# A Strassen-form input projection for a hybrid decoder trunk on one Trainium2 core

## The chip, the cores and the metric

The kernel runs on one core of a Trainium2 chip. The metric is the device time of one execution in microseconds (us); the number compared is the median over several runs. A profiled execution gives the trace. PE is the tensor engine, DVE the vector engine, ACT the scalar engine, POOL the GpSimd engine, and SP the engine that issues most transfers.

## What is computed

One layer and a final norm, in float32, for 512 tokens (`SEQ`) of width 2048 (`D_MODEL`):

```python
h = rmsnorm(x, norm_g)
proj = h @ w_in                      # 2048 x 15360
a_u, a_b, a_c, a_z, b_v, b_g, b_z, c_u, c_z, gates = split(proj)   # nine of 1024, then 6144
y_a = (silu(a_z) * (a_b * causal_dwconv3(a_c * a_u))) @ w_br_a     # 1024 x 2048
v = causal_dwconv31(b_v * sigmoid(b_g)) + conv_b
y_b = (silu(b_z) * silu(layernorm(v))) @ w_br_b
y_c = (silu(c_z) * (grouped(pooled(c_u) - c_u) * scale)) @ w_br_c  # windows 2, 4, 8, 16
g = sigmoid(gates)                                                 # three of 2048
x = x + (g0 * y_a + g1 * y_b + g2 * y_c) @ w_o                     # 2048 x 2048
return rmsnorm(x, final_g)
```

The input projection is 2048 x 15360 per token, the three branch projections are 1024 x 2048 each, and the output projection is 2048 x 2048.

## The kernel before

Every product is made in three passes. Both operands are cut into a part of 12 significant bits (`h`) and the exact rest (`l`), and the tensor engine adds `h*h`, `h*l` and `l*h` into one PSUM bank. For the weights this cut is done on the chip, chunk by chunk: a chunk is 128 x 512 numbers, ACT copies it to `wh` (L79) and DVE subtracts that from the raw chunk to give `wl` (L80). The class `Weights` runs ahead of the use: raw units of two chunks (512 KB) are loaded by the SP queue (L66) into three buffers, and the parts lie in four buffers for each of `wh` and `wl`. There are 644 chunks, each used for 12 matmuls of 512 columns.

The input projection is made with channels on the partitions. `product(x)` (L175) makes one tile of 128 channels by 512 tokens: the weight chunk is the stationary operand, 128 x 128 at a time, and the 16 tiles of `x` (as `xh`, `xl`) move past it. So a tile costs 16 x 3 = 48 matmuls, and the 120 tiles of the projection cost 5760. Channels on the partitions are what the convolutions along tokens and the per-channel parameters need, so nothing has to be turned. The reciprocal root of the mean square, which varies along tokens, is a row `R` spread over all partitions.

The order is: the head (the first four tiles, while `x` comes in), branch B up to its gate, branch A with its gates and its projection, branch B's gate and projection, branch C, and the output projection, which is made with tokens on the partitions (L479 to L481: `mh`, `ml` are stationary and the weight chunk moves). The long convolution (31 taps on DVE, L264) is put into a queue `todo` as 31 tasks a tile; `feed` takes one or two of them after each weight chunk, so they run beside the matmuls of the following products. All intermediate results stay in SBUF. The last column group of the output is made token tile by token tile, so that only one tile's norm, scaling and store lie behind the last matmul.

The order on each engine is set by a scheduler that follows the order of the program, with a priority for the cuts of the weights.

Of the kernel before, what the change touches and what calls it, by code (L numbers as in the profile page):

```python
# [19 lines left out]
NT = S // P  # L20
CONV_A = 3
# [6 lines left out]
UNIT = 2 * CH  # L28
# [3 lines left out]
# Column offsets of the segments of the input projection, in tiles of 128.  # L32
A_U, A_B, A_C, A_Z, B_V, B_G, B_Z, C_U, C_Z, GATE = (KB * i for i in range(10))

# Columns of the packed per-channel parameters.
# [9 lines left out]
HEAD = (B_V, B_G, B_V + 1, B_G + 1)  # L45


class Weights:
    """The weights in the order of their use: raw tiles are loaded ahead, and split ahead into a
    part of 12 significant bits and the exact rest, which the tensor engine takes in one pass each."""  # L50

    def __init__(self, tc, nc, raw, parts, src, load_ahead, split_ahead):
        self.tc, self.nc, self.raw, self.parts, self.src = tc, nc, raw, parts, src
        self.load_ahead, self.split_ahead = load_ahead, split_ahead
        self.fine = 1
        self.units, self.chunks = {}, {}
        self.n_units = src.shape[0]
        self.loaded = self.split = self.at = 0

    def load_to(self, n):  # L60
        while self.loaded < min(n, self.n_units):
            u = self.loaded
            t = self.raw.tile([P, UNIT], F32, tag="raw", name=f"raw{u}")
            for i in range(0, UNIT, CH if u < self.fine else UNIT):
                at = slice(i, i + (CH if u < self.fine else UNIT))
                self.nc.sync.dma_start(out=t[:, at], in_=self.src[u][:, at])  # L66
            self.units[u] = t
            self.loaded += 1

    def split_to(self, n):  # L70
        while self.split < min(n, 2 * self.n_units):
            c = self.split
            self.load_to(c // 2 + 1 + self.load_ahead)
            raw = self.units[c // 2][:, (c % 2) * CH : (c % 2 + 1) * CH]
            pool, tag = self.place(c)
            h = pool.tile([P, CH], F32R, tag=tag or "wh", name=f"wh{c}")
            l = pool.tile([P, CH], F32R, tag=tag or "wl", name=f"wl{c}")
# [4 lines left out]
            if c % 2:  # L82
                del self.units[c // 2]
            self.split += 1

    def place(self, c):
        return self.parts, None
# [8 lines left out]
def trunk(ctx: ExitStack, tc: tile.TileContext, xT, xn, wts, par, fg, out):  # L96
    nc = tc.nc
    const = ctx.enter_context(tc.tile_pool(name="const", bufs=1))
    xp = ctx.enter_context(tc.tile_pool(name="xp", bufs=2 * KD))
    up = ctx.enter_context(tc.tile_pool(name="up", bufs=2 * KB))  # L100
    vp = ctx.enter_context(tc.tile_pool(name="vp", bufs=2 * KB))
    mp = ctx.enter_context(tc.tile_pool(name="mp", bufs=KD))
    raw = ctx.enter_context(tc.tile_pool(name="raw", bufs=3))
    parts = ctx.enter_context(tc.tile_pool(name="parts", bufs=4))
    tp = ctx.enter_context(tc.tile_pool(name="tp", bufs=6))
    sp = ctx.enter_context(tc.tile_pool(name="sp", bufs=4))
# [9 lines left out]
    def tmp():  # L116
        return tp.tile([P, S], F32, tag="t", name=nm("t"))

    def psum():
        return ps.tile([P, S], F32, tag="ps", name=nm("ps"))  # L120

    def small():
        return sp.tile([P, 1], F32, tag="s", name=nm("s"), bufs=16)

    # ---- loads of the start
    gcol = const.tile([P, KD], F32, name="gcol")
    nc.scalar.dma_start(out=gcol, in_=par[:, P_G : P_G + KD])
    prm = const.tile([P, NPAR], F32, name="prm")
    xraw = []
    w = Weights(tc, nc, raw, parts, wts, 2, 3)  # L130
    for k in range(KD):
        t = mp.tile([P, S], F32, tag="m", name=f"xraw{k}")
        nc.sync.dma_start(out=t, in_=xT[:, k, :])
        xraw.append(t)
        w.load_to({0: 1, 2: 2, 4: 3}.get(k, 0))
        if k == KD - 1:
            nc.sync.dma_start(out=prm, in_=par)
# [5 lines left out]
    # The activation table and the tensor engine's full clock are had before the first data arrive.  # L143
# [4 lines left out]
    # 1 / (t + 1), for the first positions, where a window is cut off.  # L148
# [3 lines left out]

    def row(name):
        return const.tile([P, S], F32, tag="row", name=name, bufs=D // S)

    R, R2, acc, a = row("R"), row("R2"), row("squares"), row("meansq")
# [4 lines left out]
    # ---- work for the other engines that is fed in between the matrix products  # L161
    todo = deque()
    rate = [1]

    def feed(n):
        for _ in range(min(n, len(todo))):
            todo.popleft()()

    def mm3(p, whl, cols, ahl, first, last):
        (wh, wl), (ah, al) = whl, ahl  # L170
        T.matmul(p, lhsT=wh[:, cols], rhs=ah, start=first, stop=False)  # L171
        T.matmul(p, lhsT=wh[:, cols], rhs=al, start=False, stop=False)  # L172
        T.matmul(p, lhsT=wl[:, cols], rhs=ah, start=False, stop=last)  # L173
# [54 lines left out]
    for k in range(KD):  # L228
# [7 lines left out]
        for i, p in enumerate(head):  # L236
            mm3(p, whl, slice(i * P, (i + 1) * P), x[k], k == 0, k == KD - 1)
# [355 lines left out]
```

## Time and profile before

| | us |
|---|---|
| median of 3 runs | 1771.6 (1771.44 to 1772.04) |
| span of the profiled execution | 1770.0 |
| PE busy | 1759.4 (99%) |
| DVE busy | 911.4 (51%) |
| ACT busy | 530.8 (30%) |

The profiled execution's own span, from its first to its last instruction, is 1770.0 us, which is 1.6 us under the median of the runs. Matmuls overlap in the records, so the busy time of PE is the union of them; the time that one matmul takes of the engine is the distance from one start to the next.

### The profile page before, as it was taken

How to read it: one execution, taken by the hardware profiler on the slowest of the kernel's cores; microseconds unless marked ns; L12 is line 12 of the kernel's file. 1: busy time of each engine (PE TensorE's matmuls, PEld its weight loads, DVE VectorE, ACT ScalarE, POOL GpSimd, SP SyncE). 2: the span in 40 equal slices, each digit the busy share in tenths (PEclk: the TensorE clock that was granted, in tenths of full speed). 3: DMA queues.
4: the chain of work that ended last, by engine and by line, in shares of the span. 5: the costliest groups of instructions: out<-in, count | busy, mean ns of one | idle time of the engine just before them, and what ended most of it. 6: DMA issues, size and time to landing. Idle time of an engine off the chain costs nothing.

```text
span 1770.0 us, 19981 instructions
## 1 busy us (share of the span) xinstructions
PE 1759.4 (99%) x7798; PEld 1459.7 (82%) x7798; DVE 911.4 (51%) x1478; ACT 530.8 (30%) x878; POOL 0.2 (0%) x4
## 2 busy tenths in 40 slices
PE   9999999999999999999999999999999999999998
PEld 7888888888888888888888888888888888888887
DVE  7899999544443367334433333345553333363343
ACT  6322222222222234223322222233332222242232
POOL 0000000000000000000000000000000000000000
PEclk9999999999999999999999999999999999999999
DMA  6333322332232322333322233322333332262342
GB/s 229 97 98 104 95 96 96 99 102 96 96 101 96 95 96 95 102 100 97 95 96 95 96 97 102 99 96 95 96 96 96 101 100 96 96 196 95 97 130 96
DMA packets 54383, 183.93 MB, mean 104 GB/s; under 512 B 6160, under 2 KB 6288, under 8 KB 54288
## 3 DMA queue, kind: packets, MB, share of 16 engines
q1 hardware_dynamic: 50112, 175.30, 30.6%
q10 hardware_dynamic: 4176, 7.35, 1.3%
q8 instruction: 61, 1.00, 0.2%
q14 instruction: 34, 0.28, 0.0%
HBM read 178.43 MB, written 4.19 MB: 103 GB/s over the span
## 4 chain that ended last, share of the span: by engine, by line
PE 99%; DMA 0%; ACT 0%; DVE 0%; issue 0%
PE ps L171 30%; PE ps L172 30%; PE ps L173 30%; PE ps L479 2%; PE ps L480 2%; PE ps L481 2%; PE ps L496 1%; PE ps L497 1%; PE ps L498 1%; DMA xraw<-xT 0%; ACT y L509 0%; PE ps L201 0%; PE ps L200 0%; ACT squares L239 0%; ACT xh L232 0%
## 5 line engine op out<-in xcount | busy, mean ns | idle before, releaser
L80 DVE TENSOR_TENSOR wl<-raw,wh 128x512 fp32r<-128x512 f32 x644 | 443.1, 689 | 596.7 <-ACT wh L79 590.5
L171 PE MATMUL ps<-xh,wh 128*128 128x512 f32 x1920 | 746.0, 390 | 1.1 <-ACT wh L79 1.1
L172 PE MATMUL ps<-xl,wh 128*128 128x512 f32 x1920 | 747.0, 390 | 0.0
L79 ACT CAST wh<-raw 128x512 fp32r<-128x512 f32 x644 | 399.6, 622 | 1154.8 <-PE ps L172 1023.6
L173 PE MATMUL ps<-xh,wl 128*128 128x512 f32 x1920 | 741.8, 389 | 0.0
L171 PEld LDWEIGHTS ps<-xh,wh 128*128 128x128 f32 x1920 | 361.0, 188 | 76.0 <-ACT wh L79 1.4
L172 PEld LDWEIGHTS ps<-xl,wh 128*128 128x128 f32 x1920 | 361.2, 188 | 75.0
L173 PEld LDWEIGHTS ps<-xh,wl 128*128 128x128 f32 x1920 | 360.7, 188 | 74.7
L264 DVE SCALAR_TENSOR_TENSOR conv<-v,prm,conv 128x497 f32<-128x497 f32 (+25 forms) x240 | 165.1, 735 | 0.0
L481 PE MATMUL ps<-wl,mh 128*128 128x512 f32 x192 | 74.8, 390 | 0.0
L479 PE MATMUL ps<-wh,mh 128*128 128x512 f32 x192 | 74.8, 390 | 0.0
L480 PE MATMUL ps<-wh,ml 128*128 128x512 f32 x192 | 74.8, 389 | 0.0
L375 DVE TENSOR_TENSOR t<-ps,R 128x512 f32<-128x512 f32 x48 | 33.2, 692 | 73.6 <-PE ps L173 73.6
L172 PE MATMUL ps<-ucl,wh 128*128 128x512 f32 x144 | 56.1, 389 | 0.0
L173 PE MATMUL ps<-uch,wl 128*128 128x512 f32 x144 | 56.1, 389 | 0.0
L171 PE MATMUL ps<-uch,wh 128*128 128x512 f32 x144 | 56.1, 389 | 0.0
L171 PE MATMUL ps<-uah,wh 128*128 128x512 f32 x128 | 49.9, 390 | 0.0
L171 PE MATMUL ps<-ubh,wh 128*128 128x512 f32 x128 | 49.9, 390 | 0.0
L173 PE MATMUL ps<-uah,wl 128*128 128x512 f32 x128 | 49.9, 389 | 0.0
L172 PE MATMUL ps<-ubl,wh 128*128 128x512 f32 x128 | 49.9, 389 | 0.0
L173 PE MATMUL ps<-ubh,wl 128*128 128x512 f32 x128 | 49.9, 389 | 0.0
L172 PE MATMUL ps<-ual,wh 128*128 128x512 f32 x128 | 49.8, 389 | 0.0
(119 smaller groups left out, 940.3 us busy)
## 6 DMA issues: line engine op xcount, KB each, us to landing
raw<-wts SPq DMA_DIRECT2D x321, 512.0 KB, 3.4
xraw<-xT SPq DMA_DIRECT2D x16, 256.0 KB, 5.8
y<-xn ACTq DMA_DIRECT2D x16, 256.0 KB, 5.4
out<-y SPq DMA_DIRECT2D x8, 256.0 KB, 3.2
out<-y ACTq DMA_DIRECT2D x8, 256.0 KB, 3.8
fgb<-fg ACTq DMA_DIRECT2D x4, 256.0 KB, 4.3
raw<-wts SPq DMA_DIRECT2D x2, 256.0 KB, 4.3
prm<-par SPq DMA_DIRECT2D x1, 160.0 KB, 4.9
```

The source lines that it names most:

```text
L79: self.nc.scalar.copy(out=h, in_=raw)
L80: self.nc.vector.tensor_tensor(out=l, in0=raw, in1=h.bitcast(F32), op=ALU.subtract)
L171: T.matmul(p, lhsT=wh[:, cols], rhs=ah, start=first, stop=False)
L172: T.matmul(p, lhsT=wh[:, cols], rhs=al, start=False, stop=False)
L173: T.matmul(p, lhsT=wl[:, cols], rhs=ah, start=False, stop=last)
L264: V.scalar_tensor_tensor(out=c[:, s:], in0=v[:, : S - s], scalar=pcol(P_BW, i * CONV_B + CONV_B - 1 - s), in1=c[:, s:], op0=ALU.mult, op1= ...
L375: V.tensor_tensor(out=g, in0=p, in1=R, op=ALU.mult)
L479: T.matmul(pt[t], lhsT=mh[:, tk], rhs=h, start=k == 0, stop=False)
L480: T.matmul(pt[t], lhsT=ml[:, tk], rhs=h, start=False, stop=False)
L481: T.matmul(pt[t], lhsT=mh[:, tk], rhs=l, start=False, stop=k == KD - 1)
L496: T.matmul(p, lhsT=mh[:, tk], rhs=h[:, at], start=k == 0, stop=False)
L497: T.matmul(p, lhsT=ml[:, tk], rhs=h[:, at], start=False, stop=False)
```

## The change

The 15360 columns of the projection are made in 15 units of two 512-column halves (left and right). For each unit `x` (tokens by 2048) and the weights (2048 by 1024) are seen as 2 x 2 blocks: two halves of the tokens, two halves of the input channels, the left and the right columns. Strassen's form (Winograd's variant) makes the four result blocks from seven block products, where the plain form takes eight.

- The operands from `x` (`make`, `operand`) are built once, during the first unit: seven of eight tiles each, for 256 tokens, with the `h` part in the left and the `l` part in the right half of one tile. They stay in SBUF and are the stationary operand; the weight chunks move.
- Of the seven weight operands two are plain loads into the pools `A` and `C`, one is a plain load into `B`, and four are made in place: a DMA issued by POOL adds a block of the weights to the raw buffer that the product before has used (`accum_op=ALU.add`). A unit has 28 raw stages of 512 KB, 12 loaded and 16 added. An add can go out only when both chunks that lay in the buffer have been cut.
- A chunk of the projection is now used for 6 matmuls (two token tiles, three passes). 500 stages give 1000 chunks to be cut, where there were 644.
- The results come out with tokens on the partitions. ACT saves a bank where a partial sum is needed later (`snap`), DVE joins it with a later bank (`join`). What needs channels on the partitions is turned by PE, four 128 x 128 transposes a tile (`turned`): 64 tiles, 256 transposes.
- Gates, convolution inputs and outputs, `cu`, `cz` and `z` are stored to DRAM by the ACT queue (`spill`) and loaded back by the SP queue (`fill`), 256 KB each.
- The queue of side tasks is fed 0.75 tasks per chunk during the projection (1.0 in the first unit and after the projection). Turns go before the other tasks.
- The mean squares of the tokens are made from a second copy of the input, `xn`, on ACT (`square`).
- All 15 units come first, then the three branch projections with the gated sum, now with tokens on the partitions, then the turn of the sum and the output projection.

The diff, cut to its core (`branch`, the convolution, the LayerNorm and the pooling are moved and fed from DRAM, with the same arithmetic):

```diff
+PRODUCTS = (
+    ("11", "A", "load", 0, 0),
+    ("s1", "A", "add", 0, 1),
+    ("s2", "A", "add", 1, 1),
+    ("s4", "B", "load", 1, 1),
+    ("s3", "B", "add", 0, 1),
+    ("12", "C", "load", 1, 0),
+    ("22", "A", "add", 1, 0),
+)
+STEPS = KD // 4
...
     def load_to(self, n):
...
+        while self.loaded < min(n, len(self.stages)):
+            tag, key, what, b = self.stages[self.loaded]
+            if what == "load":
+                t = self.pools[tag].tile([P, RAW], F32, tag=tag, name=f"raw{tag}{self.loaded}")
+                self.nc.sync.dma_start(out=t, in_=self.src[b])
+                self.raw[key] = t, self.loaded
+            else:
+                t, before = self.raw[key]
+                assert self.split >= 2 * before + 2
+                self.nc.gpsimd.dma_start(out=t, in_=self.src[b], accum_op=ALU.add)
...
-    raw = ctx.enter_context(tc.tile_pool(name="raw", bufs=3))
-    parts = ctx.enter_context(tc.tile_pool(name="parts", bufs=4))
+    ra = ctx.enter_context(tc.tile_pool(name="ra", bufs=STEPS))
+    rb = ctx.enter_context(tc.tile_pool(name="rb", bufs=STEPS))
+    rc = ctx.enter_context(tc.tile_pool(name="rc", bufs=2))
+    parts = ctx.enter_context(tc.tile_pool(name="parts", bufs=5))
+    tp = ctx.enter_context(tc.tile_pool(name="tp", bufs=21))
...
+    w = Weights(tc, nc, {"A": ra, "B": rb, "C": rc}, parts, wts, 3, 3)
...
+    def operand(name, k, src):
+        t = slot(F32R, f"x{name}")
+        A.copy(out=t[:, half[0]], in_=src)
+        V.tensor_tensor(out=t[:, half[1]], in0=src, in1=t[:, half[0]].bitcast(F32), op=ALU.subtract)
+        sets[name][k] = t
...
+    def square(t, c):
+        x = tmp("xq")
+        nc.sync.dma_start(out=x, in_=xn[t, :, c * CH : (c + 1) * CH])
+        A.activation(out=x, in_=x, func=AF.Square, accum_out=squares[:, 4 * t + c : 4 * t + c + 1])
...
+        def run(name, banks, start):
+            for k in range(KB):
+                if first:
+                    make(name, k)
+                h, l = w.next()
+                x = sets[name][k]
+                for i, p in enumerate(banks):
+                    xh, xl = (x[:, o + i * P : o + (i + 1) * P] for o in (0, HT))
+                    T.matmul(p, lhsT=xh, rhs=h, start=start and k == 0, stop=False, skip_group_check=True)
+                    T.matmul(p, lhsT=xl, rhs=h, start=False, stop=False, skip_group_check=True)
+                    T.matmul(p, lhsT=xh, rhs=l, start=False, stop=k == KB - 1, skip_group_check=True)
+                feed()
...
+        def join(banks, r, half, ts, then):
+            for i, (p, t) in enumerate(zip(banks, ts)):
+                s = col(r, i + 2 * half)
+                if first:
+                    A.activation(out=t, in_=t, func=AF.Copy, scale=s)
+                V.scalar_tensor_tensor(out=t, in0=p, scalar=s, in1=t, op0=ALU.mult, op1=ALU.add)
+                then(i, t)
+
+        X = [psum("X") for _ in range(2)]
+        run("11", X, True)
+        a = snap(X, Rp, 0)
+        Z = [psum("Z") for _ in range(2)]
+        run("s1", Z, True)
+        e = snap(Z, Rn, 1)
+        run("s2", X, False)
+        u = snap(X, Rn, 0)
+        run("s4", Z, False)
+        if first:
+            roots()
+        join(Z, Rn, 0, u, on12)
+        run("s3", X, False)
+        join(X, Rn, 1, e, on22)
+        Z = [psum("V") for _ in range(2)]
+        run("12", Z, True)
+        join(Z, Rp, 0, a, on11)
+        run("22", X, False)
+        for i, p in enumerate(X):
+            on21(i, p, col(Rp, i + 2))
...
+    def turned(tiles, j):
+
+        p = psum("turned")
+        for t in range(NT):
+            T.transpose(out=p[:, t * P : (t + 1) * P], in_=tiles[t][:, j * P : (j + 1) * P], identity=ident)
+        return p
...
+    def prod_done(c, got):
+        def one(j):
+            i = 4 * c + j
+            p = turned(got, j)
+            t = tmp("ca")
+            V.tensor_scalar(out=t, in0=p, scalar1=pcol(P_AW, i * CONV_A + 2), scalar2=None, op0=ALU.mult)
+            for s in (1, 2):
+                V.scalar_tensor_tensor(
+                    out=t[:, s:], in0=p[:, : S - s], scalar=pcol(P_AW, i * CONV_A + 2 - s), in1=t[:, s:],
+                    op0=ALU.mult, op1=ALU.add,
+                )
+            ca[i] = t
+
+        urgent.extend(lambda j=j: one(j) for j in range(4))
```

The seven products run in the order of `PRODUCTS`; in the units with a product of two segments (`glu`, `prod`, `side`: the first six) DVE also multiplies the left by the right half.

## Rows read from the trace of the kernel before

**Rows 1.** The page: busy time of the engines, and the span in 40 slices.
```profile
PE 1759.4 (99%) x7798; PEld 1459.7 (82%) x7798; DVE 911.4 (51%) x1478; ACT 530.8 (30%) x878; POOL 0.2 (0%) x4
...
PE   9999999999999999999999999999999999999998
PEld 7888888888888888888888888888888888888887
DVE  7899999544443367334433333345553333363343
ACT  6322222222222234223322222233332222242232
```
**Rows 2.** The page: the chain that ended last, by engine.
```profile
PE 99%; DMA 0%; ACT 0%; DVE 0%; issue 0%
```
**Rows 3.** Busy time by stretch: us, PE, PEld, DVE, ACT, POOL, clock, DMA share, GB/s.
```profile
530.00:1560.00 1030.00, 1030.00 (x4546) 853.38 (x4545) 443.60 (x705) 306.52 (x495) 0.00 (x0) 1.00 0.30 97
...
44.00:310.00 266.00, 266.00 (x1175) 220.34 (x1174) 251.02 (x396) 70.00 (x113) 0.00 (x0) 1.00 0.31 98
1749.84:1760.00 10.16, 10.16 (x86) 10.15 (x85) 4.13 (x12) 2.77 (x7) 0.00 (x0) 1.00 0.32 105
```
**Rows 4.** The tensor engine's start in order of time: start, length, what.
```profile
1.04 3.78 PE L147 MATMUL ps<-ones 128*128 128x128 f32 x16 [1.04 <-DVE ones L140]
...
5.90 2.08 PE L171 MATMUL ps<-xh,wh 128*128 128x512 f32 x4 [1.08 <-ACT wh L79]
```
**Rows 5.** Groups of instructions: busy us, mean ns, then idle time before them.
```profile
L80 DVE TENSOR_TENSOR wl<-raw,wh 128x512 fp32r<-128x512 f32 x644 | 443.1, 689 | 596.7 <-ACT wh L79 590.5 <-PE ps L480 5.5 <-PE ps L172 0.3
L79 ACT CAST wh<-raw 128x512 fp32r<-128x512 f32 x644 | 399.6, 622 | 1154.8 <-PE ps L172 1023.6 <-PE ps L480 80.6 <-issue 11.7
L264 DVE SCALAR_TENSOR_TENSOR conv<-v,prm,conv 128x497 f32<-128x497 f32 (+25 forms) x240 | 165.1, 735 | 0.0
L431 DVE SCALAR_TENSOR_TENSOR t<-ps,prm,t 128x512 f32<-128x512 f32 x8 | 6.0, 751 | 1.1 <-DVE t L221 0.5
L221 DVE TENSOR_TENSOR t<-t,t 128x512 f32<-128x512 f32 x24 | 16.6, 692 | 1.7
L356 DVE TENSOR_SCALAR t<-t,prm 128x512 f32<-128x512 f32 x8 | 3.8, 480 | 0.0
L461 DVE TENSOR_TENSOR t<-ps,y 128x256 f32<-128x256 f32 x2 | 0.8, 424 | 6.7 <-PE ps L498 6.7
L232 ACT ACTIVATE xh<-xraw,gcol 128x512 fp32r<-128x512 f32 x16 | 11.2, 713 | 0.2 <-DMA xraw<-xT 0.2
L464 ACT ACTIVATE t<-t 128x512 f32<-128x512 f32 x15 | 9.5, 632 | 19.8 <-DVE t L461 19.3 <-DVE s L467 0.5
L464 ACT ACTIVATE t<-t 128x256 f32<-128x256 f32 x2 | 0.8, 417 | 7.4 <-DVE t L461 7.4
L464 ACT ACTIVATION_READ_ACCUMULATOR t<-t 128x1 f32 x17 | 3.2, 186 | 0.0
```
**Rows 6.** Transfers of the first 44 us: GB/s in 40 slices of 1.1 us.
```profile
GB/s 0 60 289 299 251 240 363 397 412 408 404 410 400 412 408 400 417 423 417 339 104 0 0 0 123 328 101 324 86 0 268 209 0 48 287 142 0 0 48 320
```
**Rows 7.** The page: the load queue as a whole, and the weight loads' time to landing.
```profile
q1 hardware_dynamic: 50112, 175.30, 30.6%
...
raw<-wts SPq DMA_DIRECT2D x321, 512.0 KB, 3.4
```
**Rows 8.** The raw weight tiles: length of an issue, and time to landing.
```profile
L66 SPq DMA_DIRECT2D raw<-wts x323: 327/328/1282, 1.2 to 1722.2; - x162
...
DMA to landing us min/median/max: 3.2/3.4/7.3
```
**Rows 9.** Waits: engine and line, what it waited for, total, times, longest.
```profile
ACT wh L79 <- PE ps L172: 1023.6, 534, 2.6
...
SPq L66 <- DVE wl L80: 1535.0, 311, 7.4
```

More of the change, by code (lines that the diff above doesn't have):

```diff
@@ L27 @@
 CH = 512
[L28 removed]
+RAW = 2 * CH
 AHEAD = 300
 WARM = 8
[L33 removed]
 P_G = 0
@@ new lines, with block, stages @@
+STEPS = KD // 4
+def block(unit, row, col, s):
+    return ((unit * 2 + row) * 2 + col) * STEPS + s
+N_UNIT = len(UNITS) * 4 * STEPS
+GW_AT = N_UNIT
+BR_AT = GW_AT + 2
+WO_AT = BR_AT + 3 * 4 * (KB // 2)
+N_BLOCK = WO_AT + 4 * (KD // 2)
+def stages():
+    out = []
+    for u in range(len(UNITS)):
+        for _, tag, what, row, col in PRODUCTS:
+            out += [(tag, (u, tag, s), what, block(u, row, col, s)) for s in range(STEPS)]
+    for n, b in enumerate(range(BR_AT, N_BLOCK)):
+        out.append(("AB"[n % 2], b, "load", b))
+    return out
@@ L58, in __init__ @@
         self.loaded = self.split = self.at = 0
     def load_to(self, n):
[L61 to L67, printed above, removed]
+        while self.loaded < min(n, len(self.stages)):
[8 more added lines that the diff above has]
+                self.nc.gpsimd.dma_start(out=t, in_=self.src[b], accum_op=ALU.add)
+                self.raw[key] = t, self.loaded
@@ L192, in halves, with rtmp @@
         return h, l
+    def rtmp(dtype, name):
+        return tp.tile([P, S], dtype, tag="t", name=nm(name))
     def total(src):
-        h, l = (tp.tile([P, S], F32R, tag="half", name=nm("half"), bufs=2) for _ in range(2))
-        A.copy(out=h, in_=src)
-        V.tensor_tensor(out=l, in0=src, in1=h.bitcast(F32), op=ALU.subtract)
+        h, l = halves(src, rtmp, "tot")
         p = psum()
@@ L328, in act @@
             V.tensor_scalar(
[L329 removed]
+                out=c, in0=c, scalar1=pcol(P_LG, i), scalar2=pcol(P_LB, i), op0=ALU.mult, op1=ALU.add
             )
[L331 to L336 removed]
@@ new lines, in side_done, with one @@
+    def side_done(c, got):
+        def one(j):
+            i = 4 * c + j
+            p = turned(got, j)
+            V.tensor_tensor(out=ca[i], in0=ca[i], in1=p, op=ALU.mult)
+            ud[i] = spill(ca[i], "ua")
+            ca[i] = None
+        urgent.extend(lambda j=j: one(j) for j in range(4))
+    gd = [[[None] * 4 for _ in range(NT)] for _ in range(3)]
+    zd = [[None] * 2 for _ in range(NT)]
+    cud, czd = ([[None] * 2 for _ in range(NT)] for _ in range(2))
+    count = {}
+    for t in range(NT):
+        for c in range(4):
+            todo.append(lambda t=t, c=c: square(t, c))
@@ new lines, in pool_tasks, with zed_tasks, load, one @@
+        todo.append(st.clear)
+    pool_tasks(0)
+    pool_tasks(1)
+    rate[0] = 1.0
+    branch(0, ua)
+    flush()
+    ub = [None] * KB
+    def zed_tasks(c):
+        st = {}
+        def load():
+            st["z"] = [fill(zd[t][c], "z") for t in range(NT)]
+        def one(j):
+            i = 4 * c + j
+            t = fill(sd[i], "sd")
+            V.tensor_tensor(out=t, in0=t, in1=turned(st["z"], j), op=ALU.mult)
+            ub[i] = halves(t, slot, "ub")
+        todo.append(load)
+        todo.extend(lambda j=j: one(j) for j in range(4))
+        todo.append(st.clear)
@@ L447, in trunk, with merge_done, one @@
+    zed_tasks(0)
+    zed_tasks(1)
+    branch(2, uc)
+    flush()
+    def merge_done(cg):
+        def one(j):
+            m[4 * cg + j] = halves(turned([merged[t][cg] for t in range(NT)], j), slot, "m")
+        urgent.extend(lambda j=j: one(j) for j in range(4))
+    branch(1, ub, merge_done)
     NG = D // CH
-    fgb = [row(f"fgb{cg}") for cg in range(NG)]
+    fgb = [slot(F32, "fgb") if cg < 2 else tmp("fgb") for cg in range(NG)]
     for cg in range(NG):
```

652 lines of the change are left out of this document (381 added, 271 removed).

## The prediction

> **What bounds the kernel now.** I read first the page's busy times and slices: PE is busy 99% of the span and full in every slice, DVE about half, ACT less than a third [rows 1]. The chain that ended last says the same from the other end: 99% of it is PE, with no stretch of transfers or waits [rows 2]. The waits show which way the engines wait: the cutting of weights waits for PE (ACT 1023.6 us), and the load queue waits for the cuts [rows 9]. So time is saved here only by giving PE less to do, and it is lost wherever something else begins to hold PE up. The price of a matmul is read from a long undisturbed stretch: 4546 matmuls in 1030 us at the full clock, 0.2266 us each [rows 3]. The last thing to see is that DVE can be very full without harm: from 44 to 310 us it is busy 251.0 of 266 us (94%) beside the long convolution, and PE shows no gap [rows 3].
>
> **What is removed.** The projection had 120 tiles x 48 = 5760 matmuls. It gets 15 units x 7 products x 8 chunks x 6 = 5040. The 720 fewer, at 0.2266, are 163.1 us. Two matmuls of the summed squares go too, 0.5 us. Branch (1152), output (768) and group products (48) keep their numbers. That the weights move and `x` is stationary costs nothing by itself: every instruction loads 128 x 128 and moves 512 columns as before.
>
> **Transposes.** 64 turned tiles x 4 = 256 PE instructions of 128 x 128 in float32. The trace has none. Below, the nearest row is the stretch from 1749.84, in which matmuls move only 256 columns: 86 in 10.16 us, 0.118 us, with the weight load busy all the time, so an instruction with its own load does not get shorter: 30 us. Above, the eight float32 products of 128 x 128 at the start, 16 records in 3.78 us: 0.47 us each; but the four matmuls after them take 2.08 us, twice what later ones take, so that stretch ran at half speed, and full speed is 0.236: 60 us [rows 3, 4]. Between ends only a factor of two apart I take the middle, 0.17 us: +44 us.
>
> **The start.** In the first unit the operands are built beside the use. Per chunk PE needs 6 x 0.2266 = 1.36 us. In the first two products ACT scales a tile (0.713), copies 256 tokens (0.417), cuts the weights (0.622) and is fed one square (0.632 + 0.186): 2.57 us, over 16 chunks 19.4 us more than PE. In s2, s4 and s3 DVE sums and cuts 256 tokens (2 x 0.424) and cuts the weights (0.689): 1.54 us, 24 x 0.18 = 4.3 us more [rows 5]. If the squares slip behind, 16 x 0.818 = 13 us of this are hidden. Bounds 10 and 27, I take +22.
>
> **DVE beside the convolution.** 1000 chunks to cut, 356 more, are 245 us more on DVE and 221 on ACT; with joins (90 of 0.751) and the rest I count some 1210 us of DVE and 860 of ACT in all, neither a bound as a mean. But 264 convolution tasks and 34 of the LayerNorm, with 24 turns ahead of them, fed at 42 a unit, fill units 1 to 8. The fullest is a side unit (there are two): 56 cuts 38.6, six joins 4.5, two products and two of the scaled kind 2.9, four silu products 2.8, four short convolutions of 0.480 + 2 x 0.75 us 7.9, 38 taps of some 0.71 us 27: 83.7 us [rows 5]. PE needs 336 x 0.2266 + 16 x 0.17 = 78.8. So 5 us too much, twice: +10. The other six stand at 73 to 76, at most 97%, near the 94% that did no harm. Bounds 0, if taps slip to later units, and 30, if each of the eight loses some 4 us.
>
> **Turns that wait.** After each of six units PE's queue holds transposes of tiles that DVE makes from the last banks (two operations of 0.751 us, behind a cut or a tap) [rows 5]. Behind a late transpose wait all following matmuls. 1.5 us each is +9; bounds 0, if the scheduler puts them later, and 18.
>
> **Transfers: plain ones.** When the load queue was full, in the eighth to nineteenth of the 40 slices of the first 44 us, it moved about 410 GB/s; 512 KB then take 1.28 us [rows 6]. As a mean over all loads the engines were busy 30.6% of 1770 us for 175.3 MB, 1.62 us for 512 KB [rows 7]. Per unit 12 loads are 15.4 us and some 16 spills and fills of 256 KB 10.2. A spill's issue (0.33 us or somewhat more [rows 8]) lies on ACT, which has room. I cost them at nothing; their cover is PE's 78.8 us a unit.
>
> **Transfers: the adds.** This is the term that decides. 240 transfers of 512 KB read DRAM and the buffer, add, and write. No row shows one. Below it costs a load, 1.28 us. Above, nothing in the trace closes the price; two loads at the mean rate are 3.24. It must move one stream more than a load, so I take two full-rate loads, 2.56 us: 16 x 2.56 = 41.0, with the plain ones 66.6 us of DMA a unit beside 78.8 of PE. Hidden, so +0. At 3.24 the sum is 77.4, still just hidden.
>
> The trace's loads move their bytes once and say nothing of an add. The Trainium skill ("Collectives: The Full Stack", Part 3, on why ReduceScatter is half of AllGather) has that the addition is free but needs two source reads on one ring, so that it runs at half the rate of a copy. By it the term would be 2.56 us again, hidden; no run here shows it yet.
>
> **The sum.** 1770.0 - 163.1 - 0.5 + 44 + 22 + 10 + 9 + 0 = 1691.4 us of span. The profiled execution lies 1.6 us under the median of the runs, so 1693. All lower ends together are 1770 - 163.6 + 30 + 10 + 0 + 0 + 1.6 = 1648, all upper ends 1770 - 163.6 + 60 + 27 + 30 + 18 + 1.6 = 1743: the likeliest case's own range.
>
> **Rival 1: an add fills the DMA engines.** If it takes three full-rate loads (3.84 us), DMA needs 87.0 us a unit, 8.2 over PE, times 15: +123, 1816 us. At four loads (5.12) it is 107.5 a unit, +430, 2123. The gain of 78.6 us is 5.2 a unit, so this decides from (78.8 + 5.2 - 25.6) / 16 = 3.65 us. For it: an unknown operation with no ceiling from a row. Against: the engines were busy only 30% [rows 7]. Chance 0.12.
>
> **Rival 2: an add is late, not wide (slower than before).** A buffer of pool A or B comes round every four stages, 8 chunks x 1.36 = 10.9 us. In it lie the wait for the second chunk's turn (1.36), its cut (0.622 + 0.689), the issue (about 0.4) and the add's time to landing L; so L may be 7.8 us. A load lands after 3.4 us, at most 7.3 [rows 5, 8]; with one more full-rate stream an add alone lands after 4.7, with twice the whole 6.8. Several in flight wait for one another, and then 7.8 is not far. Twelve stages a unit (s1, s2, s3) hang on this loop; each gets (L - 7.8) / 4 longer, so the gain of 5.2 a unit is gone at L = 9.5 us. At 12 us it is 12.6 a unit, +189: 1882 us. Against: the cuts run up to four chunks ahead, a store of some 4 us for each burst. What waits behind a late add: the cut on ACT and DVE, and behind that snaps, joins and taps, in order. Chance 0.19.
>
> On the issuing side the trace has only that DVE is 94% busy for long and that its one-input form takes 0.480 us where the two-input one takes 0.692 [rows 3, 5]. The Trainium skill ("SBUF — State Buffer", "Who interferes with whom") says that a DVE instruction in a two-port mode keeps GpSimd from writing descriptors, while a two-input tensor operation does not. By it few instructions of this kernel would hold an add up, and the chance of this rival stays as it is; no run here shows it.
>
> **Rival 3: only PE's own work counts.** Start, DVE and turns hide, transposes at the lower end: 1770 - 163.6 + 30 + 1.6 = 1638. The full DVE from 44 to 310 us speaks for it, the ACT count of the start against it. Chance 0.08.
>
> **Rival 4: DVE becomes the bound in units 1 to 8.** It is in order, and joins, taps and cuts come in bursts; if all eight lose 8 us in place of 10 in all, +54: 1747. Against: the 94% row. Chance 0.07.
>
> **How the numbers follow.** The likeliest case has 0.54: 1693 us, between 1648 and 1743. The measurement of this kernel tells a change of about 0.2% from none (3.5 us). Faster: the likeliest, rivals 3 and most of 4, together 0.65. Same: 0.04, from rivals 1 and 4 near their point of decision. Slower: the rest, 0.31, rivals 1 and 2. The range leaves out most of rival 3 below and the far part of rivals 1 and 2 above: 1645 to 1860.
>
> **What would show it.** Right: matmuls of the projection 0.227 us apart, 7,060 of 256 or 512 columns in all where there were 7,782; transposes 0.12 to 0.24 us; an add landing in under 7.8 us; PE's waits nearly all in the first 90 us and in the two side units. Wrong: the cuts (ACT) waiting for adds in s1, s2 and s3 of every unit, at a DMA share near 1 (rival 1) or well under it (rival 2); PE waiting for `wl` with DVE at 100% in units 1 to 8 (rival 4); granted clock under 1 because of gaps.

## The result, and the profile after

The changed kernel takes 1693.1 us (median of 4 runs, 1691.05 to 1697.33) beside 1771.68 us: ratio 0.9559, 95% interval 0.9545 to 0.9572. The forecast was 1693, with a range of 1645 to 1860. The sum came out, but several of its terms did not, in both directions, and this section shows where.

The page first: busy times, slices, queues, the chain by engine, then the landing time of most of the adds (us, median).

```profile
PE 1642.6 (97%) x7332; PEld 1353.5 (80%) x7332; DVE 1126.3 (67%) x1873; ACT 823.6 (49%) x1436; POOL 208.3 (12%) x246
...
PE   5899999999999999899999999999899999999997
...
DMA  9979898897989899999899898989854854443312
...
q0 software_dynamic: 34560, 125.84, 40.0%
q1 hardware_dynamic: 59616, 177.24, 32.8%
...
PE 92%; DMA 5%; DVE 1%; ACT 1%; issue 1%; SPq 0%; ACTq 0%; DVEq 0%
...
rawA<-wts POOLq DMA_DIRECT2D x180, 512.0 KB, 7.5
```

PE is still the chain, 92% of it where it was 99% [rows 2], and its slices show dips that before did not have [rows 1]: the first two, the seventeenth (676 to 718 us) and the twenty-ninth (1182 to 1225). DMA, 0.30 to 0.32 in the stretches of [rows 3], is now near 0.9 until 1200 us. Over the span the queues took 79% of the engines' time, and half of it, 40.0%, is the adds (q0).

The next view gives busy time by stretch: the first unit; the second to the eighth; the ninth; one of the later gate units; the entry to the branches. Columns as in [rows 3].

```profile
8.16:112.88 104.72, 85.47 (x336) 67.84 (x337) 73.16 (x163) 79.78 (x179) 14.79 (x17) 0.89 0.93 253
112.88:659.40 546.52, 546.28 (x2452) 450.85 (x2451) 481.83 (x763) 277.36 (x468) 96.81 (x112) 1.00 0.91 213
659.40:748.10 88.70, 81.14 (x340) 64.17 (x339) 67.73 (x106) 53.35 (x90) 13.84 (x16) 0.96 0.99 272
824.20:900.40 76.20, 76.20 (x338) 63.09 (x337) 42.34 (x63) 42.78 (x71) 13.85 (x16) 1.00 0.95 221
1204.00:1224.00 20.00, 14.08 (x52) 11.14 (x51) 10.42 (x16) 10.36 (x18) 0.00 (x0) 0.83 0.95 326
```

The fourth line is the unit as it was meant: 336 matmuls at 0.2266 us are 76.1, and it takes 76.2. The loss is read off the others. First unit: 104.72 - 76.2 = 28.5. Second to eighth: 546.52, less 2352 matmuls (533.0) and 96 transposes (10.7, price below), 2.8. Ninth: 88.7 - 76.2 = 12.5. Entry: 20.0 less 52 x 0.2266 = 8.2. The first product begins at 8.16 where it began at 5.90 [rows 4]: 2.3.

Only part of this is time in which PE stands. It is idle for 19.3 us of the first unit (104.72 less 85.47 busy), for 7.6 of the ninth and for 5.9 at the entry. The other 9.3, 4.9 and 2.3 us are matmuls that took longer, in stretches whose granted clock is 0.89, 0.96 and 0.83: a gap is paid for once more behind it.

The price of a transpose, from PE's records in order of time at 1224 us (start, length, what):

```profile
1224.48 0.60 PE L431 MATMUL turned<-ident,cu 128*128 128x128 f32 x4
1224.83 0.48 PE L642 MATMUL y<-wh,uah 128*128 128x512 f32 x1
1225.15 0.40 PE L643 MATMUL y<-wh,ual 128*128 128x512 f32 x1
```

The record of one transpose is 0.27 us long, but what it costs is what it moves the rest by. From the first of four to the second matmul behind them it is 1225.15 - 1224.48 = 0.67 us; one matmul in it is 0.227; so four cost 0.44, 0.11 each. (The matmul right behind must be taken in: it starts after 0.35 us, and the next one 0.32 behind it.) Over all 256, worked out in the same way, it is 28.5 us, 0.111 each.

Together: 1770.0 - 163.6 + 28.5 (transposes) + 28.5 + 2.3 (start) + 2.8 + 12.5 + 8.2 = 1689.2; the profiled span is 1689.3.

**Where the start waits.** PE and ACT, then SP's queue, each in order of time:

```profile
28.69 0.80 PE L338 MATMUL X<-wh,x 128*128 128x512 f32 x1 [10.65 <-ACT wh L125]
```

```profile
17.89 0.72 ACT L286 ACTIVATE xb<-xb,prm 128x512 f32<-128x512 f32 x1 [2.17 <-DMA xb<-xT]
...
23.34 4.01 ACT L286 ACTIVATE xb<-xb,prm 128x512 f32<-128x512 f32 x6 [1.53 <-DMA xb<-xT]
28.02 1.66 ACT L125 CAST wh<-rawA 128x512 fp32r<-128x512 f32 x3 [0.66 <-DMA rawA<-wts]
```

```profile
8.58 6.42 SPq L195 DMA_DIRECT2D xb<-xT  x7
17.88 0.33 SPq L105 DMA_DIRECT2D rawA<-wts  x1
```

The fourth weight stage of the first product is issued at 17.88, behind the eight tiles of the second half of `x`; ACT meanwhile takes the scalings of those tiles in its order, and the cut that PE needs starts at 28.02. PE waits 10.65 us.

**Where the ninth unit waits.** DVE, POOL, ACT, and PE's wait in that stretch:

```profile
697.47 3.35 DVE L254 RECIPROCAL rstd<-nt 128x512 f32<-128x512 f32 x1 [0.17 <-ACT nt L253]
```

```profile
702.25 0.86 POOL L110 DMA_DIRECT2D rawB<-wts  x1 [3.80 <-DVE wl L126]
```

```profile
704.71 1.14 ACT L125 CAST wh<-rawB 128x512 fp32r<-128x512 f32 x2 [3.73 <-DMA rawB<-wts]
...
712.34 1.24 ACT L351 ACTIVATE snap<-X,Rn 128x512 f32<-128x512 f32 x2
```

```profile
PE X L338 <- ACT snap L351: 5.8, 1, 5.8
```

A reciprocal of the LayerNorm holds DVE for 3.35 us, so a cut is late, so an add is late: POOL idles 3.80 us before it, where adds 2.72 us apart (a gate unit, see e8) leave 1.86. Three cuts in a row then wait on ACT for adds (only the first is shown), behind them stands a snap, and PE waits 5.8 us for the bank that it frees. This is the chain that rival 2 described ("behind that snaps, joins and taps, in order"), at the one place behind the start where PE pays for it.

**Where the entry waits.** SP's queue, then PE:

```profile
1205.03 0.33 SPq L105 DMA_DIRECT2D rawB<-wts  x1
1205.41 5.36 SPq L180 DMA_DIRECT2D ua<-ua  x7
```

```profile
1204.81 0.39 PE L340 MATMUL X<-wl,x 128*128 128x512 f32 x1
1211.12 2.08 PE L642 MATMUL y<-wh,uah 128*128 128x512 f32 x4 [5.92 <-ACT uah L235]
1212.99 0.63 PE L643 MATMUL y<-wh,ual 128*128 128x512 f32 x1
1213.42 0.63 PE L644 MATMUL y<-wl,uah 128*128 128x512 f32 x1
...
1217.22 0.39 PE L643 MATMUL y<-wh,ual 128*128 128x512 f32 x1
1217.45 0.39 PE L644 MATMUL y<-wl,uah 128*128 128x512 f32 x1
```

The fills of the first branch's input stand in the program behind the last unit, and in the in-order load queue behind weight loads that wait for their buffers. After the wait the matmuls start 0.43 us apart, and 0.23 apart six microseconds later: the clock's 1.2 and 2.4 GHz levels, and the granted 0.83 of the fifth window.

### The profile page after: what moved, and what is told of

It reads as the page before. It is cut to its first block, busy times and chain, and to the rows that moved or that the text cites. A ratio compares the mean times of both kernels' runs of the same rounds, so it can differ in the third digit from the quotient of the medians.

```text
span 1689.3 us, 21512 instructions
## 1 busy us (share of the span) xinstructions
PE 1642.6 (97%) x7332; PEld 1353.5 (80%) x7332; DVE 1126.3 (67%) x1873; ACT 823.6 (49%) x1436; POOL 208.3 (12%) x246
## 4 chain that ended last, share of the span: by engine, by line
PE 92%; DMA 5%; DVE 1%; ACT 1%; issue 1%; SPq 0%; ACTq 0%; DVEq 0%
PE X L338 12%; PE X L339 12%; PE X L340 12%; PE Z L338 6%; PE Z L340 6%; PE Z L339 6%; PE y L642 5%; PE y L644 5%; PE y L643 5%; PE V L340 3%; PE V L338 3%; PE V L339 3%; PE o L810 3%; PE o L812 3%; PE o L811 3%; PE turned L431 2%
## 5 line engine op out<-in xcount | busy, mean ns | idle before, releaser
L126 DVE TENSOR_TENSOR wl<-rawA,wh 128x512 fp32r<-128x512 f32 x560 | 379.7, 687 | 263.3 <-ACT wh L125 227.8
L125 ACT CAST wh<-rawA 128x512 fp32r<-128x512 f32 x560 | 342.4, 621 | 393.3 <-PE X L339 88.9
L126 DVE TENSOR_TENSOR wl<-rawB,wh 128x512 fp32r<-128x512 f32 x320 | 217.9, 688 | 178.5 <-ACT wh L125 146.2
L125 ACT CAST wh<-rawB 128x512 fp32r<-128x512 f32 x320 | 196.1, 622 | 266.3 <-PE y L643 67.4
L338 PE MATMUL X<-wh,x 128*128 128x512 f32 x480 | 188.8, 396 | 14.3 <-ACT wh L125 10.8
L338 PE MATMUL X<-wh,xs 128*128 128x512 f32 x480 | 189.3, 394 | 11.5 <-ACT snap L351 5.8
L338 PE MATMUL Z<-wh,xs 128*128 128x512 f32 x480 | 187.4, 393 | 3.3 <-ACT xs L269 3.1
L339 PE MATMUL X<-wh,xs 128*128 128x512 f32 x480 | 188.4, 393 | 0.0
L339 PE MATMUL X<-wh,x 128*128 128x512 f32 x480 | 187.9, 392 | 0.0
L339 PE MATMUL Z<-wh,xs 128*128 128x512 f32 x480 | 187.6, 391 | 0.0
L340 PE MATMUL Z<-wl,xs 128*128 128x512 f32 x480 | 172.9, 391 | 0.8 <-DVE wl L126 0.8
L340 PE MATMUL X<-wl,x 128*128 128x512 f32 x480 | 172.2, 394 | 0.0
L338 PEld LDWEIGHTS X<-wh,xs 128*128 128x128 f32 x480 | 91.1, 190 | 33.0 <-ACT wh L125 8.1
L340 PEld LDWEIGHTS X<-wl,xs 128*128 128x128 f32 x480 | 90.8, 189 | 20.7 <-DVE wl L126 1.8
L339 PEld LDWEIGHTS X<-wh,xs 128*128 128x128 f32 x480 | 91.1, 190 | 18.9
```

Source lines behind the costliest of these rows:

```text
L125: self.nc.scalar.copy(out=h, in_=raw)
L126: self.nc.vector.tensor_tensor(out=l, in0=raw, in1=h.bitcast(F32), op=ALU.subtract)
L338: T.matmul(p, lhsT=xh, rhs=h, start=start and k == 0, stop=False, skip_group_check=True)
L339: T.matmul(p, lhsT=xl, rhs=h, start=False, stop=False, skip_group_check=True)
L340: T.matmul(p, lhsT=xh, rhs=l, start=False, stop=k == KB - 1, skip_group_check=True)
```

## The experiments

Every run changes the kernel after the change; times are for the whole kernel, to be held against its 1693.1. e5, e6 and e7 ran four times and e12 five times, and their times are medians; the others ran once. Each trace is of one execution, and the parts differ between traces: in kernels that leave the unit in question alone the first takes 104.7 to 106.0 us, the second 77.8 to 82.6 and the ninth 88.7 to 92.0.

**e1: plain loads in place of adds.** The weight sums are left out; queue, order and number of transfers stay.

```diff
-                self.nc.gpsimd.dma_start(out=t, in_=self.src[b], accum_op=ALU.add)
+                self.nc.gpsimd.dma_start(out=t, in_=self.src[b])
```

> The 240 accumulating transfers only overwrite the buffer (the weight sums are left out), from the same queue, with the same buffers and waits. Theory: the DMA engines are the near bound (0.94 of the time in the gate units, 0.99 in the unit with the LayerNorm, 0.93 of 104.7 us in the first). Then a gate unit stays at 76.2 us with a DMA share near 0.70, the LayerNorm's unit falls from 88.7 to 77-79 us and the first from 104.7 to 82-92 us: a span near 1660 us. Rival (the first unit is bound by ACT, as the prediction had it, and the LayerNorm's unit by DVE's reciprocal): the first unit stays over 100 us, the LayerNorm's unit over 84, a span of 1680 us or more.

Measured: 1677.5 us. By stretch, the first unit, the ninth and a later gate unit:

```profile
7.90:106.30 98.40, 84.79 (x336) 66.92 (x337) 73.26 (x163) 79.67 (x179) 9.17 (x17) 0.91 0.77 273
651.40:734.70 83.30, 80.08 (x339) 65.22 (x339) 67.84 (x107) 54.34 (x90) 8.49 (x16) 0.96 0.84 292
810.90:887.10 76.20, 76.20 (x338) 63.12 (x337) 42.44 (x62) 42.80 (x71) 8.49 (x16) 1.00 0.70 221
```

Both theories miss. That a transfer adds costs 13.5 us of span (1689.3 - 1675.8, one trace each): 6.3 in the first unit, 5.4 in the ninth, the rest in small pieces, and nothing in a later gate unit, although DMA's share there falls from 0.95 to 0.70. The transfers of one gate unit, after the change and here:

```profile
q0 software_dynamic: 2301, 8.38, 60.0%
...
rawA<-wts POOLq DMA_DIRECT2D x12, 512.0 KB, 7.4
```

```profile
q0 software_dynamic: 2294, 8.35, 36.6%
...
rawA<-wts POOLq DMA_DIRECT2D x12, 512.0 KB, 4.7
```

60.0% of 76.2 us over 16 transfers is 2.86 us of the engines for an add; 36.6% is 1.74 for a plain load on the same queue.

**e2: extra copies.**

```diff
                 self.nc.gpsimd.dma_start(out=t, in_=self.src[b], accum_op=ALU.add)
+                if self.loaded % 2:
+                    d = self.tc.dram_tile([P, RAW], F32, name=f"copy{self.loaded}")
+                    self.nc.gpsimd.dma_start(out=d, in_=self.src[b])
```

> Every second add is followed by a 512 KB copy from DRAM to DRAM, on the same queue, whose result nobody reads: 8 a unit more. Theory (DMA engines 0.94 full, 4.9 us a unit to spare): at 1.67 us a copy, as for a load, 13.4 us more a unit, so a gate unit gets 76.2 + 13.4 - 4.9 = 84.7 us, and the whole about 15 x 8.5 more, 1800-1820 us. Rival (the engines have room as in the prediction's sum of 66.6 us a unit, and only an add's time to landing counts): 80.0 us of DMA a unit, 4 us a unit more at most, under 1755 us.

Measured: 1867.5 us, but not what was meant: the copies wait for nothing, so they all ran in the first unit, which took 280 us. What room the gate units have was asked again with e11.

**e3 and e4: squares without their loads, and loads without their squares.** The first takes the squares of a constant tile and loads no `xn` for them (the row sums are left out); the second loads them whole and squares one column of each tile (most of the sums are left out).

```diff
-        nc.sync.dma_start(out=x, in_=xn[t, :, c * CH : (c + 1) * CH])
-        A.activation(out=x, in_=x, func=AF.Square, accum_out=...)
+        A.activation(out=x, in_=flat, func=AF.Square, accum_out=...)
```

> The sixteen squares of the first unit are taken of a constant tile: the loads of xn (16 x 256 KB) are left out, ACT's work stays. Theory (the first unit is bound by DMA): the first unit falls from 104.7 to 90-94 us. Rival (bound by ACT, the prediction's step): it stays within 3 us of 104.7.

```diff
-        A.activation(out=x, in_=x, func=AF.Square, accum_out=...)
+        A.activation(out=x[:, :1], in_=x[:, :1], func=AF.Square, accum_out=...)
```

> The loads of xn stay, but ACT squares one column of each (the sum of squares is left out): ACT has some 10 us less. Theory (DMA): the first unit stays within 3 us of 104.7 us. Rival (ACT): it falls to 92-96 us.

Measured: 1690.0 and 1698.9 us. The first unit took 101.2 and 108.6, the second 80.6 and 82.4 beside 78.2. The 4 MB alone are worth 3.5 us of the first unit, just over the 3 that the rival allowed and far from the 11 to 15 of the theory. ACT's work for the squares alone is worth nothing: without it the first unit is longer than in any run that leaves it alone.

**e5: the fourth stage before the second half of x.**

```diff
-        if k in (0, 2, 4):
+        if k in (0, 2, 4, 6):
             w.load_to(k // 2 + 1)
```

> The fourth weight stage of the first product is loaded before the second eight x tiles instead of behind them; nothing else changes. Order theory: the unit that starts (104.7 us against 76.2 for 336 matmuls) loses time because this load is issued only at 17.88 us, behind eight loads that land after some 13 us, and ACT, in order, sits in the scaling of those tiles from 17.9 to 28; the gap of 10.8 us at 17.65 should shrink to under 4, the first unit to about 95 to 98, the whole to about 1684 to 1687. Rival, total transfer: the bytes of the start have to come anyway, and the next wait takes the gap's place: first unit 102 or more, whole 1690 or more.

Measured: 1695.0 us (1692.74 to 1700.99). PE's longest wait fell from 10.65 us to 4.5, and four others of 2.4 to 3.9 stand beside it; the first unit took 104.70, as before. The order theory falls. The chain of that run goes through 17.1 us of transfers of the second half of `x`, which now come later.

**e9 and e10: two costs of the start at once.** Plain loads (e1) together with the constant squares (e3), and together with no squares at all.

```diff
-                self.nc.gpsimd.dma_start(out=t, in_=self.src[b], accum_op=ALU.add)
+                self.nc.gpsimd.dma_start(out=t, in_=self.src[b])
...
-        nc.sync.dma_start(out=x, in_=xn[t, :, c * CH : (c + 1) * CH])
-        A.activation(out=x, in_=x, func=AF.Square, accum_out=...)
+        A.activation(out=x, in_=flat, func=AF.Square, accum_out=...)
```

> Two loads of the start at once: adds are plain overwrites (the weight sums are left out) and the squares are taken of a constant tile, so that the x rows are not loaded for them (their sums are left out); ACT does all that it did. Singly these gave a first unit of 98.4 and 101.2 us against 104.7. Transfer theory: the start is bound by bytes, the two add up or more, first unit 88 to 94. Rival, operands: ACT's and DVE's in-order building of the operands holds it, as the prediction counted (76.2 + 22): first unit 97 or more.

```diff
-    for t in range(NT):
-        for c in range(4):
-            todo.append(lambda t=t, c=c: square(t, c))
```

> As the run with plain overwrites and no x rows, and the sixteen squares themselves are left out too (some 13 us of ACT; weight sums and row sums are left out). Transfer theory: no more falls than in that run, within 2 us. Operand theory: with the squares gone the prediction's count leaves 0.39 x 16 + 4.3 = 11 us over PE's 76.2, first unit about 87, and 8 to 10 us less than with the squares. If both runs stay over 97, neither counts and the chain through DVE's sums in order is left.

Measured: 1676.7 and 1673.2 us; first unit 98.3 and 94.2 (the latter gave 1.6 back in the second unit, 79.2 beside 77.7). e9 came out where its rival had it (97 or more). In e10 neither theory holds: 4.1 us fell, where one allowed 2 and the other wanted 8 to 10. The first 64 us in two stretches for the kernel after the change, the second stretch for e1 and e3, then e9 (second stretch) and e10:

```profile
8.00:29.00 21.00, 10.19 (x37) 8.05 (x38) 6.14 (x13) 14.45 (x28) 2.74 (x3) 0.74 1.05 322
29.00:64.00 35.00, 26.41 (x89) 19.44 (x89) 31.61 (x83) 30.38 (x86) 6.20 (x8) 0.84 1.05 292
```

```profile
29.00:64.00 35.00, 28.07 (x107) 21.11 (x106) 33.03 (x89) 31.58 (x90) 3.53 (x7) 0.90 0.73 270
```

```profile
29.00:64.00 35.00, 29.05 (x107) 22.10 (x107) 32.21 (x85) 28.77 (x76) 7.93 (x10) 0.88 0.83 188
```

```profile
29.00:64.00 35.00, 30.82 (x118) 24.22 (x117) 32.36 (x89) 31.36 (x82) 4.52 (x9) 0.88 0.48 162
```

```profile
8.00:29.00 21.00, 15.21 (x47) 11.89 (x48) 10.23 (x21) 16.41 (x31) 3.27 (x6) 0.86 1.04 410
29.00:64.00 35.00, 29.63 (x123) 22.42 (x123) 33.80 (x88) 31.48 (x79) 4.14 (x8) 0.99 0.49 165
```

Until 29 us the share is 1.04 or more with and without adds; with plain loads the engines move 409 and 410 GB/s there (e9, e10), which is what the full load queue moved in [rows 6]. From 29 us the share is 1.05 with both the adds and the loads of `xn`; it is 0.73 without the adds (e1), 0.83 without those loads (e3) and 0.48 without either (e9). DVE is 90% busy in that stretch after the change and 97% in e10. The gains do not add up: e1 took 6.3 us off the first unit and e3 3.5, but both together 6.4. The squares' work was worth nothing with the rest in place (e4) and 4.1 us once the adds and the loads were gone (e10 beside e9). This fits a start with one limit behind another, transfers and then DVE with ACT, but that order is argued, not shown. By difference the adds cost 6.3 us of the 28.5 and the squares' work about 4 (2.5 net); the other 18 stand in a run without either. How they divide between the loads of `x` and the making of the operands was not separated.

**e6: LayerNorm thinned.** Empty tasks (`rest = [lambda: None] * 6`) in the queue behind each `center` and each `act`.

```diff
             todo.append(lambda i=i: center(i))
+            todo.extend(rest)
...
             todo.append(lambda i=i: act(i))
+            todo.extend(rest)
```

> Six empty tasks behind each of the sixteen LayerNorm steps that fill, work on and spill a tile, so that the same work is spread over some two units more. Theory: the unit at 659 to 748 us takes 88.7 in place of 76.2 because fills, spills and adds fill its DMA (share 0.99) and one late add holds the cuts back, with snaps behind them; thinned, no unit after the eighth takes more than 79 and the whole falls by 9 to 12 us, to 1681 to 1684. Rival: the loss belongs to the serial chain of the LayerNorm itself (reciprocal of 3.35 us on DVE, table loads), and is only moved: some unit still takes 84 or more, the whole stays over 1688.

Measured: 1681.8 us (1680.97 to 1685.79), 11.3 less. The ninth unit, the tenth and the eleventh:

```profile
663.70:741.50 77.80, 76.86 (x337) 62.83 (x336) 46.24 (x72) 42.99 (x76) 13.84 (x16) 1.00 0.97 258
741.50:818.10 76.60, 76.60 (x339) 63.43 (x338) 54.72 (x82) 48.43 (x80) 13.86 (x16) 1.00 0.99 249
818.10:894.30 76.20, 76.20 (x337) 63.08 (x337) 48.44 (x76) 44.22 (x76) 13.83 (x16) 1.00 0.97 251
```

Of the loss of 12.5 us, 1.6 is left in the ninth unit and 0.4 in the tenth, at a DMA share of 0.97 to 0.99. So the share was not the cause; what it takes is side work packed so densely that cuts come late (DVE was busy 67.7 us in the ninth unit, and is 46.2 here). The reciprocal itself is still there, in the tenth unit, and costs next to nothing. The edit also spreads the LayerNorm's fills and spills; whether those or DVE's work count for more was not separated, and e1 shows that the length of the adds has a part in it (83.3).

**e7: the first branch's input early.**

```diff
-    for i in range(KB):
-        t = fill(ud[i], "ua")
-        ua.append(halves(t, slot, "ua"))
...
+            for _ in range(16):
+                todo.append(lambda: None)
+            for i in range(KB):
+                todo.append(lambda i=i: early(i))
+                todo.append(lambda: None)
...
+    def early(i):
+        t = fill(ud[i], "ua")
+        ua.append(halves(t, slot, "ua"))
```

> The eight fills of the first branch's input and their halves are made as tasks in the last unit of the projection in place of behind it. Theory: PE's waits at the entry of the branches (some 9.6 us from 1205 us on, PE for ua from ACT, the fills issued by the in-order load queue behind weight loads that wait for their buffers) go, and the whole falls by 8 to 10 us, to 1683 to 1685; the last unit stays under 79. Rival: the fills only join a DMA that is 0.94 busy beside the adds, and the last unit pays what the entry saves: whole 1690 or more.

Measured: 1686.9 us (1685.14 to 1690.91), 6.2 less. The entry's wait is gone: the first matmul of the branch starts at 1211.10 us, 0.23 behind the last one of the projection. The last unit pays 1.5 of it (77.7 us, with one wait of 1.2 for a cut). The 8 to 10 us that were expected did not come in full.

**e8: one stage less ahead.**

```diff
-    w = Weights(tc, nc, {"A": ra, "B": rb, "C": rc}, parts, wts, 3, 3)
+    w = Weights(tc, nc, {"A": ra, "B": rb, "C": rc}, parts, wts, 2, 3)
```

> Weights are loaded and added two stages ahead instead of three, so each add has 2.72 us less to land; no byte more is moved. By the prediction's loop an add may then take 7.8 - 2.7 = 5.1 us. Late-add theory: adds land after 7.1 to 7.5 us in the gate units, 2.2 us too late, spread over four stages 0.55 us for each of twelve stages: a gate unit takes some 83 us instead of 76.2, and the whole some 90 to 100 us more, about 1790. Rival, store: the cuts that run up to four chunks ahead hide it: a gate unit under 78, whole under 1710. If adds land sooner because fewer are in flight, the loss lies between.

Measured: 1698.5 us (its second unit took 82.4); gate units 76.2. The 5 us more lie in the second and the ninth unit (91.2), within what those two differ by in other runs. It is no test of lateness after all. POOL in a gate unit that starts at 824.2 after the change, and at 831.0 in this run:

```profile
824.50 0.86 POOL L110 DMA_DIRECT2D rawA<-wts  x1 [2.09 <-DVE wl L126]
```

```profile
831.27 0.86 POOL L110 DMA_DIRECT2D rawA<-wts  x1 [2.08 <-DVE wl L126]
```

The adds go out at the same place in the unit (0.30 and 0.27 us after its start, then every 2.72). POOL's queue holds little but adds, and each waits for DVE's cut of its buffer, so when the program names it makes no difference.

**e11: three times the spills in the gate units.**

```diff
                 gd[b][t][2 * h] = spill(o, "g")
+                for _ in range(2):
+                    spill(o, "more")
```

(and the same for the right half)

> Each of the eight tiles that a gate unit writes out is written twice more, to buffers that nothing reads: 16 writes of 256 KB a unit, issued by ACT behind the first, so in step with the unit. At 0.75 us of the DMA engines each that is 12 us beside the 71.5 us (share 0.94) that a gate unit has now. Full theory (prediction's rival 1, an add fills the engines): the share goes to 1, a gate unit takes about 83.5 us in place of 76.2, six of them cost 44 us, whole about 1735. Rival, a busy engine is not a full one: the unit moves 221 GB/s now and would move 276, which the unit at 659 us reached with 272; the rows' time per packet shrinks, adds land a little later, and a gate unit stays under 78, whole under 1705.

Measured: 1699.4 us. The ninth unit and the tenth:

```profile
659.50:756.60 97.10, 84.05 (x339) 66.14 (x338) 68.32 (x106) 53.80 (x90) 13.83 (x16) 0.93 0.98 277
756.60:832.80 76.20, 76.20 (x338) 63.08 (x337) 40.92 (x62) 41.35 (x71) 13.83 (x16) 1.00 1.04 280
```

The tenth unit's transfers:

```profile
rawA<-wts POOLq DMA_DIRECT2D x12, 512.0 KB, 8.3
...
rawB<-wts POOLq DMA_DIRECT2D x4, 512.0 KB, 9.2
```

A quarter more bytes cost a gate unit nothing, though adds land after 8.3 and 9.2 us; the rival was right that a share of 0.95 is not full. All of the 6 us, and more, is in the ninth unit (97.1 beside 88.7, and 92.0 at most in runs that leave it alone), where the LayerNorm's work lies too.

**e12: the two gains together.**

> The two edits that gained by themselves together: LayerNorm steps thinned by six empty tasks each (1681.8 alone against 1693.1) and the first branch's input made in the last unit of the projection (1686.9 alone). Theory, that they are two separate waits: 1693.1 - 11.3 - 6.2 = 1675.6, or up to 2 us less since the entry's wait was a little longer in the thinned run; ratio to the kernel before about 0.945. Rival, that the thinned LayerNorm pushes its transfers into the last unit beside the early fills: over 1680.

The edits are those of e6 and e7. Measured: 1676.9 us (1675.63 to 1679.87), ratio to the kernel before 0.947, interval 0.9457 to 0.9483, and so below the changed kernel's too. The entry:

```profile
1190.00:1210.00 20.00, 20.00 (x90) 16.57 (x89) 11.91 (x19) 10.90 (x18) 0.00 (x0) 1.00 0.90 316
```

The ninth unit takes 78.8 us and the entry's wait is gone, and the gains add up to within 1.3 us of 11.3 + 6.2.

## Why the prediction was right, and which of its steps were not

**PE's own work: right.** The matmuls are as many as forecast (7332 records less 256 transposes and 16 of the warm-up: 7060), and a unit without other losses takes 336 x 0.2266 = 76.2 us.

**Transposes: over-sized.** 28.5 us for +44, just under the lower end of 30. The row of 256-column matmuls at 0.118 us was the right neighbour. The upper row came from a start at half speed, and the middle between the two was no better for being the middle.

**The start: under-sized, and costed by the wrong cause.** +22 was written, some 31 came, over the upper bound of 27. The prediction had ACT bound in the first two products at 2.57 us a chunk, with the squares as a part of it. But squares left out alone gave nothing (e4). The step that failed is to cost the start by one engine's sum and the transfers at nothing: "their cover is PE's 78.8 us a unit" does not hold in the first unit, which takes 6.3 us less with plain loads for the adds (e1) and 3.5 less without the loads of `xn` (e3). By difference the adds are 6.3 of the 28.5 us and the squares' work about 4; the other 18, of `x` and its operands, stay undivided. Nor did the sum hold a term for the lower clock behind the gaps, 9.3 us of the 28.5.

**DVE beside the convolution and waiting turns: over-sized.** +10 and +9 were written; the second to the eighth unit lost 2.8 us together. The fullest units are the two side units, as forecast; this is the first of them, the fourth unit:

```profile
269.53:348.32 78.79, 78.74 (x355) 64.67 (x354) 73.86 (x119) 39.28 (x67) 14.25 (x17) 1.00 0.89 199
```

Its 119 instructions on DVE are about the 120 that the prediction counted, but they keep DVE busy for 73.9 us and not 83.7. What failed is the price: the lengths of single records were added, 0.70 us in the mean, while the records overlap their neighbours and an instruction takes 0.62 us of the engine (three cuts in a row stand in the trace with 1.82 us, 0.61 each, at a record length of 0.69). [rows 3] had it already, 251.02 / 396 = 0.63. The reason given for the bound of 0 counts for less: 33 taps ran in that unit where 38 were counted, and none behind the eighth unit.

**The adds: hidden, as written.** An add takes 2.86 us of the engines, not 2.56, still under the 3.65 from which rival 1 would decide, and e11 shows that even more bytes stay hidden in gate units. Beside a plain load on the same queue an add takes 2.86 / 1.74 = 1.6 times as long. The Trainium skill ("Collectives: The Full Stack", Part 3) has ReduceScatter, which adds, run at half the rate of a copy; by the measured 1.6 that rule is on the right side and somewhat too dear.

**Rival 2: its limit too strict, its chain real.** 7.8 us of landing was to be the point from which a unit grows. Adds land after 7.1 to 7.5 us in the median, which alone would settle nothing; but with 8.3 and 9.2 (e11) a gate unit still takes 76.2. An add's issue takes 0.86 us and not 0.4, so the limit as reckoned would even have been 7.4. The twelve stages without an add and the store of cut chunks give time back, which the division by four did not count (argued, not tried: e8 did not delay any add). Where DVE was crowded as well, in the ninth unit, the chain came as described and cost 12.5 us. On the issuing side POOL's 240 adds took 853 to 1008 ns each, so no long hold-up shows. This agrees with what the Trainium skill ("SBUF — State Buffer", "Who interferes with whom") says of two-input tensor operations, that they do not keep GpSimd from writing descriptors.

**Not in the sum at all: 20.7 us.** The LayerNorm beside a gate unit (12.5, nearly all of it removed by e6) and the in-order load queue at the entry of the branches (8.2, mostly removed by e7). None of PE's waits was to lie there ("nearly all in the first 90 us and in the two side units"), and the side units have next to none; one of the signs of being wrong, a granted clock under 1 because of gaps, was there in all three places. The prediction costed spills and fills by their bytes only; the entry's fills are cheap in bytes and late in order. These two and the start's excess (31 for 22) came out against the transposes, DVE and turns, 32 us too dear. The hit on the total is therefore partly luck.

**Open.** Why the second unit takes 77.8 to 82.6 us in runs that do not touch it, was not found. What holds the other 18 us of the start was not found either.

## What to carry to other kernels

When work is taken off the bounding engine, cost the places where it changes hands (the first unit, the passage from one phase to the next, a block of side work that meets a new one) by each in-order queue, not by bytes or by an engine's mean: in this kernel all 52 us that were lost beyond the transposes lay there, and next to nothing in the 1000 us between. A high DMA share says that engines hold packets, not that no more fit; to know whether transfers bound a stretch, add some to it and see whether it grows. When an edit alone gives nothing, try it once more behind another before its theory is dropped: the squares' work gave nothing in e4 and 4.1 us in e10. And do not add up gains that were measured one by one: 6.3 and 3.5 us of the start came to 6.4 together (e1, e3, e9), while 11.3 and 6.2 at two separate places came to 16.2 of 17.5 (e12). Last, when an engine's work is summed up, price an instruction by the distance between starts, not by the length of its record.

## What the hardware showed that was not expected

- In a gate unit an accumulating transfer of 512 KB took 2.86 us of the DMA engines beside 1.74 for a plain one on the same queue, and landed after 7.4 us beside 4.7; its issue takes 0.86 us of POOL.
- At a DMA share of 0.95 and 221 GB/s a unit had room for 280 GB/s without an effect on PE; the share then reads 1.04.
- A 128 x 128 float32 transpose amid 512-column matmuls cost 0.111 us, though its record is 0.27 long.
